# Modulation products of the second layer placed between latent-attention items, their weights split on GpSimd

## The chip, the cores and the metric

The kernel runs on one core of a Trainium2 chip. The metric is device time in microseconds of one execution. The engines are TensorE (PE in the profile; PEld is its weight load), VectorE (DVE), ScalarE (ACT), GpSimd (POOL) and the sequencer that issues most loads (SP).

## What is computed

Two models run one after the other on 512 tokens of width 1024: a block with sparse attention, a memory cross-attention and a feed-forward of width 4096, and then two layers of a mixer that also carry 256 context tokens. The part that the change touches is the modulation of the two mixer layers. It depends on the two condition vectors alone, so it can be computed at any time before its layer uses it:

```python
sc = jax.nn.silu(c)
scc = jax.nn.silu(c_ctx)
for i in range(DEPTH_2):                       # two layers
    mod_x = sc @ w_mod[i] + b_mod[i]           # (1024) x (1024, 3072)
    mod_c = scc @ w_mod[i] + b_mod[i]
    x, ctx = mixer_layer(x, ctx, mod_x, mod_c, ...)
```

In each layer shift and scale of the modulation enter the first norm, and its gate enters the last step. Between them a layer has a window attention, a short convolution, and a latent attention of 8 heads over 768 keys (512 tokens and 256 context tokens).

## The kernel before

All products keep float32 accuracy: each operand is split into a high and a low part, and a product is three matmuls (high by high, low by high, high by low). The kernel is one list of steps, `ops`. Each step is a generator that issues work for one block of weights, and after each piece of it a clock of estimated time (`tick`) lets loads, splits of coming weights and background generators (attention above all) issue theirs. The finished program is then put in order per engine by a scheduler with a timing model of its own, so instructions of neighbouring steps are interleaved, and each engine works through its own fixed order.

Weights come through `Stream`. SP loads chunks of 512 KB into "raw" buffers. `pump` then splits the next unit in stream order into `wh` and `wl`, from a ring of 9 buffers (`RING`). For blocks with `fr=True`, as the modulation's, a unit is 128 rows by 512 columns: ScalarE copies it to `wh` (L266) and VectorE subtracts to get `wl` (L267). Other blocks get float16 halves with a scale; those with `pool=True` have their high half made by GpSimd (L271) and their low half by VectorE (L291).

One modulation product, `mod(i, j, blk)` (L1439), computes 512 of layer `i`'s 3072 columns, for both conditions at once. It takes 8 units. Each has two matmuls over 512 columns, one with 34 stationary columns (L1444 or L1447) and one with 2 (L1445). Then ScalarE and VectorE add the two parts (L1451, L1452) and ScalarE's queue writes the row to DRAM (L1453). After the sixth product of a layer `mod_chain` (L1458) starts: six small loads on ScalarE's queue, a few small VectorE operations (the first is L1469), one matmul and one GpSimd power for a scale (`total`), and three stores to DRAM (L1486). `mod_bc` later reads these with a broadcast load.

Where the 12 products stand is written as the string `MODS`, one letter per product. Before, all six of the second layer (`i` = 1) come first. In order of time: one after the projections of the gating unit (`d`), two after the gating unit (`u`), three while the memory attention runs in the background (`h`). Of the first layer (`i` = 0) one more stands at `h`, two at `i` behind the memory output projection, and three inside the feed-forward (after its parts 0, 1 and 2). After part 4 of the feed-forward `ctx_norm0` norms the context tokens and reads the first layer's modulation for it.

Latent attention is the generator `b_items` (L1932) run by `attention`. For each head it yields five items (four query tiles of 128 over 768 keys, one of two context tiles over 256), and between them small projections: the next head's queries (`qb_head`), the next pair of keys (`kb_pair`), values, gate pieces (`extra`). An item's steps are the score matmuls into one of two PSUM buffers `S`, a maximum on VectorE (L705), an exponential on ScalarE (L721), transposes into one of three PSUM buffers `mm` (L734), a split of these on ScalarE and VectorE (L738, L739), and the value matmuls (L755). All projections and modulation products use the same three `mm` buffers.

## Time and profile before

| | |
|---|---|
| median of 3 runs | 2425.56 us (2424.42 to 2427.5) |
| the profiled execution | 2421.47 us |
| its span, first to last instruction | 2419.7 us |
| PE busy | 2261.3 us, 93% |
| DVE busy | 1544.2 us, 64% |
| ACT busy | 1298.1 us, 54% |
| POOL busy | 320.7 us, 13% |
| mean granted TensorE clock | 0.978 |

The span stands 1.8 us below the time of its own execution, and that execution 4.1 us below the median. Busy shares are means over stages with different limits, so each stage is read by itself. The feed-forward lies at about 480 to 850 us, latent attention of the first layer at about 1165 to 1330 us.

### The profile page before, as it was taken

The page shows a single profiled execution, that of the slowest core. Times are in us where ns is not written, and L with a number is a line of the kernel's source. Part 1 is how long each engine was busy: PE and PEld are TensorE (multiplying, and loading weights), DVE is VectorE, ACT ScalarE, POOL GpSimd, SP SyncE. Part 2 cuts the span into 40 slices and gives each one's busy share as a digit, 9 for nine tenths or more (in the row PEclk, how much of TensorE's full clock was granted, in tenths as well). Part 3 has the DMA queues.
Part 4 walks back from the last instruction along what each step waited for, and adds up shares of the span by engine and source line. Part 5 has one row for each costly group of instructions (what it writes and reads, how often), then busy time and mean ns, then how long its engine had stood idle before and what let it go on. Part 6 is the DMA issues. An engine that isn't in the chain of part 4 may idle for free. (4 is left out here: it accounts for less than half of the span.)

```text
span 2419.7 us, 38066 instructions
## 1 busy us (share of the span) xinstructions
PE 2261.3 (93%) x14342; PEld 1505.2 (62%) x14342; DVE 1544.2 (64%) x3136; ACT 1298.1 (54%) x2745; POOL 320.7 (13%) x703
## 2 busy tenths in 40 slices
PE   7899899899999989999988999999779999899998
PEld 6777687544444557767767566557546567764446
DVE  6878678656665677665777444443777657865543
ACT  5656457746655455535777434323535457775532
POOL 4320321100100211004000000000621121000001
PEclk9899899899999999999999999999989999999999
DMA  4512445534443411112221422211421113233311
GB/s 158 140 47 71 141 144 199 172 101 153 155 140 106 122 50 38 46 40 65 79 74 56 137 79 61 79 42 63 156 86 50 42 38 108 71 115 113 103 44 61
DMA packets 182220, 226.67 MB, mean 94 GB/s; under 512 B 28556, under 2 KB 130876, under 8 KB 182036
## 3 DMA queue, kind: packets, MB, share of 16 engines
q1 hardware_dynamic: 158084, 187.67, 25.1%
q10 hardware_dynamic: 23952, 36.57, 4.4%
q8 instruction: 112, 1.84, 0.3%
q14 instruction: 72, 0.59, 0.1%
HBM read 207.33 MB, written 16.88 MB: 93 GB/s over the span
## 5 line engine op out<-in xcount | busy, mean ns | idle before, releaser
L416 PE MATMUL mm<-hTh,wh 128*128 128x512 f16 (+1 forms) x1040 | 392.6, 378 | 7.3 <-ACT wh L273 3.1
L291 DVE SCALAR_TENSOR_TENSOR wl<-raw,gs,wh 128x512 f16<-128x512 f32 (+2 forms) x420 | 296.6, 751 | 150.6 <-ACT wl L224 116.5
L417 PE MATMUL mm<-hTl,wh 128*128 128x512 f16 (+1 forms) x1040 | 392.4, 377 | 0.0
L418 PE MATMUL mm<-hTh,wl 128*128 128x512 f16 (+1 forms) x1040 | 391.2, 377 | 0.0
L224 ACT ACTIVATE wl<-raw 128x1024 f16<-128x1024 f32 (+3 forms) x242 | 222.9, 921 | 69.6 <-PE mm L417 37.3
L416 PEld LDWEIGHTS <-wh 128*128 128x128 f16 x1712 | 168.0, 98 | 147.4 <-issue 6.8
L417 PEld LDWEIGHTS <-wh 128*128 128x128 f16 x1712 | 168.0, 98 | 146.1 <-issue 9.6
L418 PEld LDWEIGHTS <-wl 128*128 128x128 f16 x1712 | 167.8, 98 | 143.9 <-issue 0.6
L738 ACT ACTIVATE ph<-mm 128x512 f16<-128x512 f32 (+2 forms) x300 | 146.1, 502 | 162.4 <-PE mm L734 156.1
L273 ACT ACTIVATE wh<-raw,gs 128x1024 f16<-128x1024 f32 x156 | 175.3, 1141 | 105.9 <-PE mm L417 83.0
L266 ACT ACTIVATE wh<-raw 128x512 fp32r<-128x512 f32 (+2 forms) x244 | 141.7, 613 | 142.2 <-PE mm L418 49.7
L739 DVE SCALAR_TENSOR_TENSOR pl<-mm,ph 128x512 f16<-128x512 f32 (+2 forms) x300 | 165.9, 567 | 73.6 <-ACT ph L738 71.1
L267 DVE TENSOR_TENSOR wl<-raw,wh 128x512 fp32r<-128x512 f32 (+2 forms) x244 | 156.1, 667 | 55.3 <-ACT wh L266 40.2
L432 POOL TENSOR_TENSOR gs<-gs,nh 128x1 f32<-128x1 f32 x66 | 40.6, 616 | 1125.2 <-DVE gs L431 1079.3
L416 PE MATMUL mm<-wh,hTh 128*128 128x512 f32 (+5 forms) x512 | 181.7, 356 | 5.5 <-DVE vf L1589 2.0
L418 PE MATMUL mm<-wh,hTl 128*128 128x512 f32 (+5 forms) x512 | 180.1, 352 | 1.8 <-DVE hTl L422 1.7
L417 PE MATMUL mm<-wl,hTh 128*128 128x512 f32 (+5 forms) x512 | 180.1, 352 | 0.3 <-DVE wl L267 0.3
L734 PE MATMUL mm<-ident,P 128*128 128x128 f32 x928 | 153.9, 283 | 5.9 <-ACT P L721 2.0
L721 ACT ACTIVATE P<-S,s 128x768 f32<-128x768 f32 (+4 forms) x160 | 105.8, 666 | 35.1 <-PE mm L734 18.0
L734 PEld LDWEIGHTS mm<-ident,P 128*128 128x128 f32 x928 | 108.6, 145 | 19.6 <-ACT P L721 2.9
L2133 DVE SCALAR_TENSOR_TENSOR z<-z,mm 128x256 f32<-128x256 f32 (+1 forms) x72 | 42.8, 596 | 107.2 <-PE mm L418 98.9
L271 POOL TENSOR_SCALAR wh<-raw,gs 128x1024 f16<-128x1024 f32 (+3 forms) x54 | 65.8, 1219 | 328.2 <-PE mm L417 209.9
(503 smaller groups left out, 5360.8 us busy)
## 6 DMA issues: line engine op xcount, KB each, us to landing
raw<-in_w_in_dram SPq DMA_DIRECT2D x124, 512.0 KB, 3.5
raw<-in_w_ff_dram SPq DMA_DIRECT2D x64, 512.0 KB, 4.5
raw<-in_w_mod_dram SPq DMA_DIRECT2D x48, 512.0 KB, 5.1
raw<-in_w_branch_dram SPq DMA_DIRECT2D x24, 512.0 KB, 3.4
raw<-in_w_o_dram SPq DMA_DIRECT2D x16, 512.0 KB, 4.0
raw<-in_cmp_w_dram SPq DMA_DIRECT2D x16, 256.0 KB, 3.5
raw<-in_w_out_dram SPq DMA_DIRECT2D x8, 512.0 KB, 3.6
raw<-in_w_mkv_dram SPq DMA_DIRECT2D x8, 512.0 KB, 3.7
```

The costliest lines, as they stand in the source:

```text
L224: nc.scalar.activation(lo[:, :b - a], t[:, a:b], AF.Square, accum_out=g.t[:, g.cols:g.cols + 1])
L266: nc.scalar.activation(hi[:, :m], src, AF.Copy)
L267: nc.vector.tensor_sub(lo[:, :m], src, hi[:, :m].bitcast(FT))
L273: nc.scalar.activation(hi[:, :m], src, AF.Copy, scale=s)
L291: self.nc.vector.scalar_tensor_tensor(l[:, b], src[:, b], s, h[:, b], op0=OP.mult, op1=OP.subtract)
L416: PE.matmul(ps, ah, bh, start=start, stop=False)
L417: PE.matmul(ps, ah, bl, start=False, stop=False)
L418: PE.matmul(ps, al, bh, start=False, stop=stop)
L721: ACT.activation(P, v[:, j, :], AF.Exp, bias=it.nb[:, j:j + 1], accum_out=it.den[:, j:j + 1])
L734: PE.transpose(ps[:, a - a0, :], it.P[0 if len(it.P) == 1 else j][:, c:c + 128], ident)
L738: ACT.activation(ph[:, :m], ps[:, :m], AF.Copy, scale=PSC)
L739: DVE.scalar_tensor_tensor(pl[:, :m], ps[:, :m], PSC, ph[:, :m], op0=OP.mult, op1=OP.subtract)
```

## The change

The change moves modulation products. `MODS` becomes six letters and lists the first layer alone: two products at `u`, two at `h`, two at `i`; none at `d` and none in the feed-forward. The six of the second layer go into the latent attention of the first layer, heads 1 to 6, product `j` = head minus 1. `mod` can now run a part of its 8 units: units 0 to 3 follow the item (head, query tile 1), units 4 to 7 the item (head, query tile 3). Its PSUM buffer is taken at unit 0 and kept to unit 7. These blocks have `pool=True`, and for them both halves of the split are GpSimd's, a copy for `wh` and a subtraction for `wl`. The small operand `s1` moves to a pool that lives through the whole kernel.

```diff
-MODS = 'duuhhhhii012'
+MODS = 'uuhhii'
@@ Stream.pump
+        elif fr and u.blk.pool:
+            nc.gpsimd.tensor_copy(hi[:, :m], src)
+            nc.gpsimd.tensor_tensor(lo[:, :m], src, hi[:, :m].bitcast(FT), op=OP.subtract)
         elif fr:
             nc.scalar.activation(hi[:, :m], src, AF.Copy)
             nc.vector.tensor_sub(lo[:, :m], src, hi[:, :m].bitcast(FT))
@@ mod_init
-        s1 = sc["one"].tile([128, 8, 34], FR, tag="ms1", name="ms1")
+        s1 = one.tile([128, 8, 34], FR, tag="ms1", name="ms1")
@@
-    def mod(i, j, blk):
-        ps = mmtile([128, 512])
-        for k in range(8):
+    def mod(i, j, blk, ks=range(8)):
+        if ks[0] == 0:
+            lay["mps"] = mmtile([128, 512])
+        ps = lay["mps"]
+        for k in ks:
...
+        if ks[-1] < 7:
+            return
@@
-    def b_items(nq, segs, blks, extra):
+    def b_items(nq, segs, blks, extra, mods):
...
+                if h in mods and qt in (1, 3):
+                    yield proj_item(mod(1, h - 1, mods[h], range(qt * 2 - 2, qt * 2 + 2)))
@@ layer
+        md = {j + 1: wblk(A["w_mod_2"][1][:, j * 512:(j + 1) * 512], fr=True, pool=True) for j in range(6)} if i == 0 else {}
...
+            bl += [md[h]] if h in md else []
@@
-    mods = [(n, (1, n) if n < 6 else (0, n - 6)) for n in range(12)]
+    mods = [(n, (0, n)) for n in range(6)]
```

## Rows read from the trace of the kernel before

**Rows 1.** Stretch, length; busy PE, PEld, DVE, ACT, POOL (instructions); clock; DMA share, GB/s.

```profile
500.00:660.00 160.00, 159.27 (x742) 71.53 (x741) 92.58 (x178) 97.27 (x172) 8.79 (x14) 1.00 0.41 126
370.00:425.00 55.00, 52.58 (x394) 39.84 (x393) 49.39 (x88) 41.92 (x96) 7.00 (x18) 0.97 0.67 227
1165.00:1200.00 35.00, 33.20 (x263) 27.52 (x261) 23.92 (x51) 25.46 (x72) 0.69 (x1) 1.00 0.23 68
1200.00:1322.00 122.00, 104.11 (x791) 87.56 (x790) 94.34 (x182) 88.65 (x191) 3.88 (x6) 0.96 0.22 69
```

**Rows 2.** Waits of PE in latent attention, 1165 to 1345 us: total, times, longest.

```profile
PE S L416 <- ACT P L721: 12.1, 11, 2.5
PE O L755 <- DVE yb L2009: 2.8, 3, 2.1
```

**Rows 3.** Timeline of PE around a product in the feed-forward: start, duration, instruction.

```profile
623.83 0.38 PE L417 MATMUL mm<-wl,ffh 128*128 128x512 f16 x1
624.05 0.38 PE L418 MATMUL mm<-wh,ffl 128*128 128x512 f16 x1
...
627.97 0.39 PE L416 MATMUL mm<-hTh,wh 128*128 128x512 f16 x1
```

**Rows 4.** Timelines of ACT's queue, DVE and PE where the context norm starts.

```profile
652.77 1.42 ACTq L1486 DMA_DIRECT2D mod_d<-mf  x1
...
660.78 1.28 DVE L618 SCALAR_TENSOR_TENSOR xn<-ctx,s,g 128x1024 f32<-128x1024 f32 x1 [4.00 <-DMA g<-mod_d]
...
654.85 0.38 PE L416 MATMUL mm<-wh,ffh 128*128 128x512 f16 x1 [0.73 <-DVE oc L1240]
663.12 0.38 PE L416 MATMUL mm<-wh,ffh 128*128 128x512 f16 x1 [2.93 <-DVE oc L1240]
```

**Rows 5.** Timelines of DVE and PE at the end of the memory attention.

```profile
411.34 4.88 DVE L267 TENSOR_TENSOR wl<-raw,wh 128x512 fp32r<-128x512 f32 x8
417.55 0.68 DVE L1452 TENSOR_TENSOR z<-mm,z 2x512 f32<-2x512 f32 x1
418.16 4.89 DVE L267 TENSOR_TENSOR wl<-raw,wh 128x512 fp32r<-128x512 f32 x8
...
419.60 0.39 PE L1447 MATMUL mm<-wh,ms 128*34 128x512 f32 x1
420.18 0.48 PE L416 MATMUL mm<-wh,moh 128*128 128x512 f32 x1
```

**Rows 6.** Busy time by stretch, at the product `d` and just behind it.

```profile
230.00:240.00 10.00, 9.64 (x121) 6.62 (x119) 9.61 (x15) 9.33 (x20) 0.00 (x0) 1.00 0.62 196
250.00:260.00 10.00, 6.07 (x44) 3.88 (x43) 4.74 (x9) 4.76 (x13) 4.49 (x15) 0.79 0.00 0
```

**Rows 7.** What VectorE's first operation of the modulation chain (L1469) waited for.

```profile
  DMA raw<-in_w_mod_dram: 3.5, 1
  DMA mf<-raw_d: 2.4, 1
```

**Rows 8.** GpSimd's wide operations, by form: count, busy us and mean ns, idle before.

```profile
L271 POOL TENSOR_SCALAR wh<-raw,gs 128x1024 f16<-128x1024 f32 x40 | 53.0, 1328 | 222.0 <-PE mm L417 127.6 <-PE mm L418 69.1 <-issue 24.4
...
L271 POOL TENSOR_SCALAR wh<-raw,gs 128x576 f16<-128x576 f32 x2 | 1.5, 748 | 7.0 <-PE mm L417 7.0
```

**Rows 9.** Timelines of POOL and DVE in the window attention, where both work at once.

```profile
876.84 3.20 POOL L271 TENSOR_SCALAR wh<-raw,gs 128x1024 f16<-128x1024 f32 x2 [18.36 <-PE mm L418]
915.65 1.12 POOL L271 TENSOR_SCALAR wh<-raw,gs 128x1024 f16<-128x1024 f32 x1 [3.60 <-PE mm L417]
...
876.94 0.42 DVE L1549 TENSOR_TENSOR y<-z,ra 128x256 f32<-128x256 f32 x1
877.28 1.26 DVE L1550 TENSOR_TENSOR y<-z,ra 128x256 f32<-128x256 f32 x1
...
902.61 0.15 DVE L1659 TENSOR_TENSOR s<-nb,sk 128x4 f32<-128x4 f32 x1
...
915.95 0.83 DVE L1659 TENSOR_TENSOR s<-nb,sk 128x4 f32<-128x4 f32 x1
```

**Rows 10.** VectorE groups with two SBUF inputs, 1200 to 1322 us: the largest two.

```profile
L291 DVE SCALAR_TENSOR_TENSOR wl<-raw,gs,wh 128x512 f16<-128x512 f32 x18 | 12.7, 746 | 0.7 <-ACT wl L224 0.7
L1863 DVE TENSOR_TENSOR qb<-y,qb 128x512 fp32r<-128x512 f32 x5 | 3.4, 681 | 0.0
```

More of the change, by code (lines that the diff above doesn't have):

```diff
@@ L2277, in layer @@
             bl += [za[f] for f in range(4) if zh.get(f) == h]
-        add(lambda *b: attention(b_items(nq, segs, [x for x in b if x not in za], zat)), *bl)
+            bl += [md[h]] if h in md else []
+        other = za + list(md.values())
+        add(lambda *b: attention(b_items(nq, segs, [x for x in b if x not in other], zat, md)), *bl)
         add(lambda: s4_start())
```

## The prediction

> **What bounds the kernel now.** I read first the busy time by stretch, then in each stretch that the change touches PE's waits and the timelines of the engines beside it. The feed-forward is bound by PE: 159.27 us of 160 [rows 1]. The end of the memory attention is bound by VectorE and PE together (49.39 and 52.58 of 55 us), and the stretch with the product at `d` likewise [rows 1, 6]. Latent attention is different: from 1200 to 1322 us PE works 104.11 of 122 us (85%), VectorE 94.34, ScalarE 88.65, and GpSimd 3.88 [rows 1]. Its largest wait is of score matmuls for the exponential that frees their PSUM buffer, 12.1 us in 11 pieces, none longer than 2.5 [rows 2]. So that stage has holes in PE and an idle GpSimd, and the feed-forward has neither; the question is how much of the moved work falls into the holes.
>
> **What a product costs on PE.** From one float16 matmul's start to the next is 0.22 us. From the last one before the third product to the first behind it is 3.92 us [rows 3]. So the product's 16 matmuls take 3.92 - 0.22 = 3.70 us, and six take 22.2 us.
>
> **Removed from the feed-forward.** Three products on a busy PE: 3 x 3.70 = 11.1 us. Their splits, loads and sums lie beside PE work and give nothing more. Bounds 9 to 11.3 (below 11.1 if the scheduler's new order opens small holes).
>
> **The wait of the context norm.** The first layer's modulation is now finished before the feed-forward. In the trace the chain's last store is issued at 652.8 us, VectorE stands 4.00 us for the broadcast load from it, and two matmuls then wait 0.73 and 2.93 us for sums queued behind that on VectorE [rows 4]. The 3.66 us should go; what is late next there are the context rows' own load and the norm, so I take 3.3, bounds 1 to 3.7.
>
> **Removed at `h` (four products to two).** Behind the memory attention's last values VectorE does two runs of 8 subtractions, 4.88 and 4.89 us, with 0.68 between, and PE's next projection starts at 420.18, right behind the fourth product [rows 5]. Two products cost 2 x 3.70 = 7.4 us on PE and about 2 x (4.9 + 0.7) = 11.2 us on VectorE. The stage is near the limit of both, so the gain lies between; but with fewer products beside it, attention's own chain shows. I take 8, bounds 4 to 11.
>
> **Removed at `d` (one product to none).** PE 9.64 and VectorE 9.61 of 10 us there [rows 6], so 3.7 us of PE or 5.6 us of VectorE. But right behind it PE is busy 6.07 of 10 [rows 6]: norm chains set the pace, and what is won may be waited away. I take 3, bounds 0 to 5. The products at `u` and `i` keep their places and only change layer.
>
> **The chain of layer one moves to the start of the feed-forward.** Its first VectorE operation waited 2.4 and 3.5 us for loads in its two uses [rows 7], with weight splits queued behind it. Bounds 0 to 3.5; the nearer use is the one inside the feed-forward, where PE still worked 159.27 of 160 us [rows 1]; I take 0.5.
>
> **Added to latent attention.** Each product brings 16 matmuls, 8 copies and 8 subtractions on GpSimd, one ScalarE copy, one VectorE add, one store on ScalarE's queue, and four loads of 512 KB on SP. The 24 loads are 12.6 MB; over some 135 us that is 93 GB/s on top of 69. The memory attention ran at 227 GB/s [rows 1], so I cost them at nothing; without that cover GpSimd's copies would wait for them.
>
> *PE.* 104.1 + 22.2 = 126.3 us of work. If every hole fills, the 122 us become 126.3: +4.3. If none fills: +22.2. The nearest row is the same stage's beginning, 1165 to 1200, where gate pieces lie between the items: PE 33.20 of 35, 94.9% [rows 1]. At that share 126.3 / 0.949 = 133.1: **+11.1**.
>
> *GpSimd's time.* Nothing in the trace shows a copy or a two-input subtraction of 512 columns there. The one-input operation takes 0.748 us for 576 columns and 1.12 undisturbed for 1024 [rows 8, 9], so 0.83 ns a column and about 0.70 us for the copy. The subtraction is bounded below by the same 0.70 and above by twice it, 1.40; with two inputs to fetch I take the upper, about 2.1 us a unit, 101 us for 48. They may begin in head 0, as far as the ring of 9 allows, so there are about 130 us: enough, if waits stay below 0.6 us a unit. Waits for the five small powers queued behind them are inside this.
>
> The Trainium skill (GPSIMD Engine Reference, Engine selection) speaks against the change: two-input elementwise work belongs on VectorE, and its cycle accounting gives some 2.6 cycles an element, by which I estimate 1.1 us for the subtraction. By it the unit is 1.8 us and the sum does not change.
>
> *VectorE beside GpSimd.* A 4-element VectorE operation with two SBUF inputs took 0.83 us instead of 0.15 while GpSimd's wide one ran; a 256-column one took 1.26 instead of 0.42; and GpSimd's two beside it took 3.20 instead of 2.24 [rows 9]. They exclude each other. From 1200 to 1322 us VectorE has 34 such operations (18 and 5 in the largest groups [rows 10]). With GpSimd busy some 80%, and half of about 1 us left on average, each waits 0.4 us: 14 us more on an engine that has 28 idle. Most are weight splits ahead of need, five are queries that scores wait for. I take **+3**, bounds 0 to 8.
>
> *The rest.* The chain of the second layer now runs at head 6: six loads and three stores on ScalarE's queue, and VectorE's wait of 2.4 to 3.5 us [rows 7] with maxima queued behind: **+1.5**, bounds 0 to 3.5. A product keeps one of three `mm` buffers from tile 1 to tile 3; transposes and key projections have two meanwhile. No row shows that; PE's waits on these buffers are small against those for `S` [rows 2], so **+1**, bounds 0 to 4.
>
> **The sum**, against the profiled execution of 2421.47 us: removed 11.1 + 3.3 + 8 + 3 = 25.4; added 0.5 + 11.1 + 3 + 1.5 + 1 = 17.1; net -8.3. The median stands 4.1 us above that execution, and I let the difference stand: 2425.56 - 8.3 = **2417**. With all parts at their best it would be 31 less against 4.3 more, 2399; at their worst 14 less against 41 more, 2453.
>
> **Rivals.**
> (a) *The holes fill almost wholly*, because the scheduler may put a ready product ahead of a score matmul that waits. For it: the holes are 1 to 2.5 us [rows 2] and half a product is 1.85. Against it: the order is fixed by a model, and real waits fall elsewhere. Then 4.3 + 2.5 is added and 25.4 removed: 2407. Chance 0.22.
> (b) *Little is won before the feed-forward.* The norm chains and the attention's own chain are as long without the products. For it: the idle behind `d` [rows 6]. Against: VectorE near full at both places. Then only 14.4 is removed against 17.1: 2428. Chance 0.20.
> (c) *GpSimd becomes the bound of latent attention (slower).* If a unit with its waits takes over (122 + 11 + 8) / 48 = 2.9 us, PE waits for weights in its fixed order. At 3.3 us the 48 take 158 us instead of 130, VectorE's collisions grow to 8, and the sum is -25.4 + 28 + 8 + 1.5 + 1 + 0.5 = +13.6: 2439. For it: the mutual exclusion [rows 9], by which a copy of 1.12 became 1.6. Against: at 2.1 us a unit there is 30% to spare. Chance 0.13. The Trainium skill's rule above points to this side; by its own figure the unit stays below the limit.
>
> **How the numbers follow.** Main case 0.45, centred on 2417, 2409 to 2425. I give 2403 to 2432: it holds the main case, nearly all of (b) and most of (a), and leaves out (c) and the far end of (a). About 0.2% (4.9 us) is what a measurement of this kernel can tell from no change. Faster by more: most of the main case and (a), 0.60; within: 0.23; slower: (c) and the upper part of (b), 0.17.
>
> **What the changed profile would show.** Feed-forward some 14 us shorter with no wait on a load from the modulation. The stretch from the last memory-attention values to the output projection shorter by about 7. Latent attention some 16 us longer with PE at 93 to 96% in its middle; if PE stays at 85%, no hole was filled. GpSimd's copies near 0.7 and subtractions at or below 1.4 us, with PE seldom waiting for them; many such waits mean (c). Waits of transposes for an `mm` buffer would show the PSUM term too small. The forecast is wrong if the stages before the feed-forward keep their length, or if latent attention grows by over 25 us.

## The result and the profile after

The changed kernel takes 2441.16 us, the kernel before, measured beside it, 2426.53: a ratio of 1.0059, 95% interval 1.0042 to 1.0077. It is slower by some 14.6 us, where 2417 and a range of 2403 to 2432 were forecast. The profiled execution took 2440.92 us (span 2439.1), that of before 2421.47 (span 2419.7); their spans differ by 19.4 us, since the profiled execution of before lay some 5 us under its median. The ledger below is between these two.

Where the time went is read from the same instruction in both traces. The sums of the feed-forward's second product first, in the kernel before (the two figures behind the durations are the first and the last start):

```profile
L1240 DVE SCALAR_TENSOR_TENSOR oc<-mm,gs,oc x64: 737/750/753, 516.1 to 825.6; 128x512 f32<-128x512 f32 x64
```

The same in the changed kernel:

```profile
L1243 DVE SCALAR_TENSOR_TENSOR oc<-mm,gs,oc x64: 736/750/754, 513.2 to 805.9; 128x512 f32<-128x512 f32 x64
```

The changed kernel is 2.9 us ahead at the first of these sums and 19.7 ahead at the last: the feed-forward is 16.8 us shorter. The same reading at other places: 6.5 us ahead at the first operation behind `d` (246.0 to 239.5), 5.4 at the first sum of the output projection (292.3 to 286.9), 7.6 at the last sum behind the memory attention (445.4 to 437.8), 4.9 at the feed-forward's first activation (478.2 to 473.3). Most of the gain of 19.7 is kept as far as latent attention, whose first maximum stands 18.3 us earlier. Then all of it is lost and more.

The rows of stretches answer to [rows 1] and [rows 4]: the changed kernel's feed-forward, the place where the context norm starts, and latent attention over the same times as before's [rows 1].

```profile
500.00:660.00 160.00, 160.00 (x750) 72.61 (x748) 91.31 (x169) 85.80 (x125) 5.39 (x9) 1.00 0.34 112
640.00:680.00 40.00, 40.00 (x188) 18.12 (x187) 21.51 (x38) 21.61 (x32) 0.55 (x1) 1.00 0.32 105
1165.00:1322.00 157.00, 131.53 (x906) 99.39 (x906) 111.69 (x197) 96.16 (x225) 87.18 (x91) 0.97 0.36 115
```

PE is now never idle where it waited 3.66 us for the context norm. In latent attention it works 131.53 of 157 us, 84%, where before it worked 33.20 + 104.11 = 137.31 of the same stretch [rows 1]: 22 us of matmuls (by the forecast's price) were added to the stage, which is also longer, and this stretch of it became emptier.

Latent attention is measured from VectorE's first maximum to its last output sum, and the ends of the first three of its four head pairs are the second reciprocal of each. These are rows of VectorE's timeline, of the kernel before:

```profile
1160.91 0.95 DVE L705 TENSOR_REDUCE s<-S 128x1 f32<-128x768 f32 x1
1202.88 0.18 DVE L2013 RECIPROCAL s<-dn 128x4 f32<-128x4 f32 x1
1248.14 0.17 DVE L2013 RECIPROCAL s<-dn 128x4 f32<-128x4 f32 x1
1297.60 0.17 DVE L2013 RECIPROCAL s<-dn 128x4 f32<-128x4 f32 x1
1335.44 0.42 DVE L2009 TENSOR_TENSOR yb<-O,yb 64x256 f32<-64x256 f32 x1
```

and of the changed kernel:

```profile
1142.62 0.96 DVE L708 TENSOR_REDUCE s<-S 128x1 f32<-128x768 f32 x1 [0.81 <-PE S L421]
1187.24 0.15 DVE L2022 RECIPROCAL s<-dn 128x4 f32<-128x4 f32 x1
1238.68 0.17 DVE L2022 RECIPROCAL s<-dn 128x4 f32<-128x4 f32 x1
1295.29 0.17 DVE L2022 RECIPROCAL s<-dn 128x4 f32<-128x4 f32 x1
1352.52 0.42 DVE L2018 TENSOR_TENSOR yb<-O,yb 64x256 f32<-64x256 f32 x1
```

The stage is 174.5 us before and 209.9 after: **35.4 us longer**. The pairs take 42.0, 45.3, 49.5 and 37.8 before, 44.6, 51.4, 56.6 and 57.2 after. Behind it little is added: the changed kernel is 17.1 us late at the stage's end, 18.3 at the first merge and 19.4 at its own end.

PE's waits in latent attention, 1165 to 1345 us, answer to [rows 2]:

```profile
PE S L419 <- ACT P L724: 7.2, 6, 3.2
PE mm L419 <- DVE pl L742: 6.3, 7, 2.7
PE mm L737 <- DVE pl L742: 3.9, 3, 2.2
PE O L758 <- ACT ph L741: 3.8, 6, 1.8
PE mm L433 <- DVE sb L431: 2.8, 2, 2.2
PE mm L2029 <- DVE pl L742: 1.4, 2, 0.8
```

PE waits no longer mostly for the exponential but for `mm` buffers that VectorE's `pl` (the low half of the transposed exponentials) frees: 11.6 us in the second, third and sixth row. No wait of PE for GpSimd stands in the whole list. GpSimd's own groups in the stage:

```profile
L267 POOL TENSOR_TENSOR wl<-raw,wh 128x512 fp32r<-128x512 f32 x45 | 58.8, 1320 | 0.5 <-ACT wl L224 0.3
L266 POOL CAST wh<-raw 128x512 fp32r<-128x512 f32 x45 | 30.7, 692 | 74.4 <-PE mm L420 27.9 <-PE mm L1452 17.5 <-PE mm L1449 10.0
```

A unit takes 0.69 + 1.32 = 2.01 us, as forecast (2.1), and GpSimd is idle 74.4 us before its copies, 55.4 of them until PE frees a ring buffer. So it is late for nobody that the profile names, and still the stage is 35 us longer. That is what the experiments are about.

### The profile page after: what moved, and what is told of

Its sections match the earlier page's. It is cut to its first block, busy times and chain, and to the rows that moved or that the text cites. A ratio compares the mean times of both kernels' runs of the same rounds, so it can differ in the third digit from the quotient of the medians.

```text
span 2439.1 us, 38037 instructions
## 1 busy us (share of the span) xinstructions
PE 2276.1 (93%) x14342; PEld 1515.8 (62%) x14342; DVE 1532.3 (63%) x3088; ACT 1273.9 (52%) x2673; POOL 415.7 (17%) x799
## 3 DMA queue, kind: packets, MB, share of 16 engines
q1 hardware_dynamic: 158084, 187.67, 24.9%
## 4 chain that ended last, share of the span: by engine, by line
PE 78%; DVE 8%; ACT 5%; DMA 3%; issue 3%; POOL 2%; SPq 0%; ACTq 0%; DVEq 0%; POOLq 0%
PE mm L419 22%; PE mm L420 21%; PE mm L421 21%; PE mm L737 3%; PE O L758 2%; DVE wl L294 2%; ACT P L724 1%; DVE pl L742 1%; ACT wl L224 1%; ACT ph L741 1%; PE S L419 1%; PE S L633 1%; DMA raw<-in_w_in_dram 1%; PE S L421 1%; PE S L420 1%
## 5 line engine op out<-in xcount | busy, mean ns | idle before, releaser
L435 POOL TENSOR_TENSOR gs<-gs,nh 128x1 f32<-128x1 f32 x66 | 40.6, 616 | 975.4 <-DVE gs L434 917.9
L269 ACT ACTIVATE wh<-raw 128x512 fp32r<-128x512 f32 (+2 forms) x196 | 114.5, 610 | 89.3 <-PE mm L420 20.1
L270 DVE TENSOR_TENSOR wl<-raw,wh 128x512 fp32r<-128x512 f32 (+2 forms) x196 | 126.1, 669 | 30.6 <-ACT wh L269 29.0
L708 DVE TENSOR_REDUCE s<-S 128x1 f32<-128x768 f32 (+4 forms) x112 | 97.5, 874 | 22.2 <-PE S L421 14.5
```

Of the source, the lines that this page charges most:

```text
L269: nc.scalar.activation(hi[:, :m], src, AF.Copy)
L270: nc.vector.tensor_sub(lo[:, :m], src, hi[:, :m].bitcast(FT))
```

## The experiments

Each figure called "stage" is the length just defined, in the profiled execution of that kernel. Kernels that leave part of the splitting out have other values in the second layer's modulation. Each stage length comes from one execution; four kernels that leave the stage as it was (the kernel before among them) have 174.4 to 175.6, so a difference of 1 to 2 us says nothing.

### What is it: buffers, splits or matmuls?

**A PSUM buffer for each half.** The half is closed with its own copy, add and store:

```diff
-        if ks[0] == 0:
-            lay["mps"] = mmtile([128, 512])
-        ps = lay["mps"]
+        ps = mmtile([128, 512])
...
```

> Each half product of the second layer gets its own PSUM buffer and is closed at once (one copy, one add, one store more per product; the chain loads both halves and adds them). The changed kernel took 2441 us, and its first latent attention grew from 174 to 210 us. Theory 'hold' (a product keeps one of three mm buffers for 17 to 22 us, so transposes and projections wait): the waits for mm buffers fall from about 20 to under 8 us, the stage to about 198, the time to 2428 to 2433. Theory 'collisions' (VectorE and GpSimd exclude each other): stage 208 to 212, time 2438 to 2444. Theory 'added work' (the matmuls fill no hole): the same, 2438 to 2444.

2438.14 us, ratio 1.0044 [1.0029, 1.0060]; stage 208.0, 1.9 less. From first matmul to copy the six products keep buffers for 80 us in all instead of 115, and others of PE's waits take the place of those for `mm` buffers. Two rows of its stage:

```profile
PE O L758 <- ACT ph L741: 8.9, 4, 4.4
PE mm L737 <- DVE pl L742: 2.7, 4, 0.8
```

The waits of `mm` for `pl` are 4.1 us in all instead of 11.6, the wait for `ph` 8.9 instead of 3.8. Not keeping the buffer across the gap brings almost nothing.

**The product whole, behind tile 1.**

```diff
-                if h in mods and qt in (1, 3):
-                    yield proj_item(mod(1, h - 1, mods[h], range(qt * 2 - 2, qt * 2 + 2)))
+                if h in mods and qt == 1:
+                    yield proj_item(mod(1, h - 1, mods[h]))
```

> The eight units of a product lie together behind tile 1 of a head instead of four behind tile 1 and four behind tile 3, so its PSUM buffer is kept some 6 us instead of 17 to 22. Theory 'hold': the stage goes from 210 to about 200 us, the time to 2430 to 2434. Theory 'collisions' and theory 'added work': no change, 2438 to 2444. Theory 'GpSimd's pace' (eight units at about 2 us each have to be split ahead): PE waits for splits and the time is 2441 to 2450.

2441.87 us, 1.0055 [1.0033, 1.0077]; stage 213.5. It did not do what it was made for: the matmuls were spread over as long as before (107 us of keeping). It only shows that the arrangement in halves matters little.

**One split in eight.** The other pieces reuse the first one's split.

```diff
+        again = fr and u.blk.pool and u.ks[0] > 0
+        if again:
+            hi, lo = u.blk.of[0][0].hi, u.blk.of[0][0].lo
...
```

> GpSimd splits only the first of the eight weight pieces of each second-layer product; the other seven matmul pairs use that split again, so 42 of 48 copies and subtractions are left out (the second layer's modulation has other values than the reference's). Matmuls, loads, buffers and their order stay. Theory 'collisions': VectorE's operations return to their durations of the kernel before, the stage goes from 210 to about 195 us, the time to 2424 to 2430. Theory 'hold' or 'added work': stage 206 to 210, time 2437 to 2442. Theory 'GpSimd's pace': as 'collisions', but then PE's waits, not VectorE's busy time, are what falls.

2412.90 us, 0.9937 [0.9917, 0.9958]; stage 185.4. All matmuls, loads and stores are there, and the stage is only 10.9 us longer than before. **The 42 splits left out cost 24.5 of the 35.4 us.** The time is below the 2424 that any theory gave, and the buffers are now kept for 37 us: GpSimd's work, the waiting and the keeping went together, so the run names the splits and not the way they cost. Part of that way can be read. The stage with one split in eight, and in the changed kernel (columns as in the rows of stretches above):

```profile
1142.78:1328.19 185.41, 169.21 (x1277) 133.10 (x1275) 135.85 (x274) 129.75 (x298) 13.09 (x16) 0.99 0.36 108
1142.62:1352.52 209.90, 178.82 (x1280) 138.23 (x1279) 151.26 (x280) 132.19 (x304) 91.87 (x97) 0.95 0.36 112
```

Of the 24.5 us PE is idle for 14.9, and for 9.6 it is longer at work on nearly the same number of matmuls. The added idle time is mostly waiting for VectorE, 18.5 us instead of 5.2; of these the waits of `mm` for `pl` are 11.6 us instead of 1.6, while those for the exponential stay. With one split in eight:

```profile
PE S L425 <- ACT P L730: 7.4, 8, 2.0
PE mm L743 <- DVE pl L748: 0.8, 4, 0.3
PE mm L425 <- DVE pl L748: 0.5, 1, 0.5
PE mm L2035 <- DVE pl L748: 0.3, 1, 0.3
```

In these waits of the changed kernel VectorE is at work for 18.1 of the 18.5 us. One of the two longest, of 2.2 us, ends with the second of these rows of VectorE's timeline:

```profile
1257.80 3.26 DVE L1919 TENSOR_TENSOR wl<-raw,wh 128x288 fp32r<-128x288 f32 x3
1261.75 0.41 DVE L742 SCALAR_TENSOR_TENSOR pl<-mm,ph 128x256 f16<-128x256 f32 x1
```

There `pl` stands in VectorE's order behind three splits of query weights. Beside GpSimd's work they took 1.50 us (288 columns) and twice 0.96 (48 columns); in the kernel before such splits take 0.45 and 0.20.

The longer work of PE goes with its granted clock, 0.95 of full speed (2.4 GHz) over the stage instead of 0.99. Behind the stretch with that wait, in which PE worked 2.10 of 4.30 us and VectorE 4.09, the clock fell to 1.2 GHz:

```profile
1259.00:1263.30 4.30, 2.10 (x16) 1.37 (x16) 4.09 (x7) 0.40 (x1) 4.30 (x5) 1.00 0.36 111
1263.30:1266.70 3.40, 3.11 (x16) 2.34 (x16) 1.60 (x3) 1.96 (x5) 3.35 (x3) 0.50 0.98 325
1266.70:1272.00 5.30, 5.25 (x50) 4.74 (x49) 3.39 (x6) 3.02 (x10) 0.00 (x0) 1.00 0.98 325
```

No run holds the clock fixed, so how many of the 9.6 us are its doing is not shown.

**Keeping a buffer alone**, in the kernel before:

```diff
+                if 1 <= h <= 6 and qt == 1 and nq == 6:
+                    lay["mps"] = mmtile([128, 512])
+                    PE.transpose(lay["mps"][:1, 0:128], st["den"][:, 1, h % 2:h % 2 + 1], ident)
+                if 1 <= h <= 6 and qt == 3 and nq == 6:
+                    PE.transpose(lay["mps"][:1, 128:256], st["den"][:, 3, h % 2:h % 2 + 1], ident)
...
```

> The kernel before, and in the first latent attention one of the three mm buffers is taken behind tile 1 of heads 1 to 6 and given back behind tile 3 (two transposes of one column and a one-element copy per head, nothing else). Theory 'hold': latent attention grows from 174 to 182 to 188 us, the time by 8 to 14 us. Theory 'collisions' or 'added work': the time grows by at most 2 us.

2439.57 us, 1.0053 [1.0039, 1.0067]; stage 190.0, 15.5 longer (a profiled execution 7 us above its median). A buffer taken from the attention is dear by itself. But own buffers, kept for 80 us instead of 115, gave back only 1.9 us of the changed kernel's 35.4.

**The last split first.** Own buffer for each half, and its matmuls begin with the piece that is split last, so that they can run together:

```diff
+        order = [ks[-1], *ks[:-1]] if i else list(ks)
+        for k in order:
...
```

> The changed kernel with a PSUM buffer for each half product (closed with one copy, one add and one store of its own, as in the run with own buffers), and the half's last split used first, so that its matmuls start when all four splits are there. Measured so far from a product's first matmul to its copy, summed over six: changed kernel 115 us, own buffers 80, one split 37, and the stage 209.9, 208.0, 185.4 us; a buffer kept for nothing in the kernel before lengthened the stage by 15.5. Theory 'hold paced by GpSimd' (the buffer is kept for as long as GpSimd needs to deliver the splits): sum of holds 25 to 40, stage 190 to 198 us, time 2420 to 2430. Theory 'collisions' (wide GpSimd operations hold VectorE up; 15.7 us in the changed kernel) or 'ring and order': stage 204 to 212, time 2434 to 2444.

2448.72 us, 1.0110 [1.0080, 1.0141]; stage 217.9. The expected shortening failed: the scheduler again spread the matmuls (96 us of keeping), and the stage grew. Over the kernels with products the stage follows the keeping only roughly: 37 us of it go with 185.4 (and 185.1), 44 with 194.2, 49 with 207.3 and with 212.1 (kernels below, whose products run in one piece), 80 with 208.0, 96 with 217.9, 107 with 213.5, 115 with 209.9, 120 with 216.8, 132 with 217.3, 154 with 255.2. From 49 to 115 it hardly grows; below that, the splitting was cut as well.

### Is it VectorE, held up by GpSimd?

**GpSimd's work alone**, in the kernel before, first without anything to wait for:

```diff
...
+                if 1 <= h <= 6 and qt < 4 and nq == 6:
+                    for _ in range(2):
+                        for _ in range(2):
+                            POOL.tensor_copy(gx, gx)
+                        for _ in range(2):
+                            POOL.tensor_tensor(gx, gx, gx, op=OP.subtract)
```

> The kernel before, and in heads 1 to 6 of the first latent attention GpSimd does as many columns of copies and subtractions as the changed kernel's 42 to 48 splits, on a tile of its own that nobody reads (two units behind each of the tiles 0 to 3; nothing waits for them). The one-split run gave 28 us of the changed kernel's time to GpSimd's splits. Theory 'collisions' (VectorE's operations are held up while GpSimd works): VectorE's busy time in the stage rises by 15 us or more, the stage grows from 174 to 185 to 195 us, the time by 10 to 20 us. Theory 'pace' (matmuls stand in a fixed order behind splits that come late): the stage stays within 3 us, the time within 4 us of the kernel before.

2428.39 us, 1.0014 [1.0004, 1.0025]. It says nothing on the question: with nothing to wait for, the operations ran ahead of the stage, which took 175.6 (the row gives the first and the last start):

```profile
L1971 POOL TENSOR_TENSOR gx<-gx x96: 607/614/1471, 839.2 to 1040.6; 128x256 f32<-128x256 f32 x96
```

**The same, held back to its place:** a first copy of one column reads the tile's sums of exponentials.

```diff
...
+                    POOL.tensor_copy(gx[:, 0:1], st["den"][:, qt, h % 2:h % 2 + 1])
...
```

> The kernel before with GpSimd's 48 units of copies and subtractions on a tile of its own, as in the run that let GpSimd run ahead, but now each pair of units waits for the exponentials of its tile of attention, so that the work lies in heads 1 to 6 of latent attention. Theory 'collisions': VectorE's busy time in the stage rises by 15 us or more, the stage from 174 to 185 to 195 us, the time to 2435 to 2445. Theory 'late splits': stage up to 178, time within 4 us of the kernel before.

2448.91 us, 1.0098 [1.0069, 1.0126], which looks like the collisions; the profile says otherwise. The stage took 179.6, 5.1 longer, and VectorE's work in it rose by 2.9 us (134.1 against 131.2). The rest came behind the stage: GpSimd was still at its backlog, and ScalarE stood 27.3 us for one load instead of 4.5 (`ACT yhl L681 <- DMA xn<-yc_d`); what held the load up I did not follow. A total without its stages would have misled here.

**Once more, with operations 512 wide and free in time** (heads 1 to 5; `gi` reads a 128-column constant four times, and the results have half the width in bytes, so the subtraction takes 1.07 us):

```diff
...
+                if 1 <= h <= 5 and qt < 4 and nq == 6:
+                    POOL.tensor_copy(gx[:, 0, 0:1], st["den"][:, qt, h % 2:h % 2 + 1])
+                    for _ in range(2):
+                        POOL.tensor_copy(gx, gi)
+                        POOL.tensor_tensor(gx, gi, gi, op=OP.subtract)
```

> The kernel before with 40 units of one 512-column copy and one 512-column subtraction on GpSimd, two behind each of the tiles 0 to 3 of heads 1 to 5, each pair held back until its tile's exponentials are done; operations as wide as the changed kernel's, and GpSimd free again before the stage ends (the earlier run of this kind used 256 columns and left a backlog at the stage's end). Theory 'collisions' (VectorE's two-input operations wait for GpSimd's, so the wider the worse): VectorE's busy time rises by 8 to 15 us, the stage from 174.5 to 184 to 195 us, time 2434 to 2445. Theory 'buffers and order': up to 178 us, time within 4 us of the kernel before.

2429.92 us, 1.0022 [1.0007, 1.0038]; stage 180.3, 5.8 longer, VectorE 3.7 us longer at work. In these two runs GpSimd works about as long in the stage as in the changed kernel (94.8 and 78.5 us against 91.9), and collisions alone cost 5 to 6 us, not 25. But they hold VectorE up for 3 to 4 us only, where the changed kernel has 15.4 us more VectorE work than with one split in eight; so the two runs do not bound what 15 us of it would cost.

**VectorE's time alone**, 48 subtractions more in the kernel before:

```diff
...
+                if 1 <= h <= 6 and qt < 4 and nq == 6:
+                    for _ in range(2):
+                        DVE.tensor_tensor(gx, gi, gi, op=OP.subtract)
```

> The kernel before with 48 subtractions of 512 columns more on VectorE (about 0.68 us each, 33 us in all), two behind each of the tiles 0 to 3 of heads 1 to 6 of the first latent attention, on data that is always there and for nobody. From the first maximum to the last output sum the kernel before takes 174.5 us there, the changed kernel 209.9. Theory 'VectorE's time' (whatever keeps VectorE longer, its own work or GpSimd's, lengthens the stage nearly one for one): 195 to 208 us, time 2444 to 2458. Theory 'buffers and order' (the splits cost through the ring of buffers and the fixed order, and VectorE has room): up to 184 us, time up to 2434.

2437.83 us, 1.0046 [1.0028, 1.0064], and inconclusive for the same reason as the first GpSimd run. The row of the added line shows when they ran:

```profile
L1968 DVE TENSOR_TENSOR gx<-ident x48: 672/688/1369, 839.1 to 914.0; 128x512 f16<-128x512 f32 x48
```

Free of waits, the scheduler put all 48 into the window attention, 320 us too early. The stage itself stayed at 174.4. (Where they landed they cost some 11 us by the ratio, 15 by the start of latent attention in the two profiled executions; that says something of that stage alone.)

**GpSimd's work in place.** The one-split kernel, and GpSimd copies and subtracts the other 42 pieces on the loaded weights themselves, for nobody:

```diff
+        elif again:
+            nc.gpsimd.tensor_copy(src, src)
+            nc.gpsimd.tensor_tensor(src, src, src, op=OP.subtract)
...
```

> The one-split kernel (2413 us), but GpSimd does the copy and the subtraction of the other 42 pieces in place on the loaded weights: the same GpSimd work at the same time, loads that wait for it, and nobody who needs its result (the second layer's modulation has other values than the reference's). Theory 'late splits' (PE stands in a fixed order behind the splits and their ring): 2413 to 2418 us, latent attention as with one split. Theory 'collisions' (VectorE is held up by GpSimd), or loads held up by GpSimd: 2433 to 2442 us; in the first case VectorE's busy time in the stage rises from 136 to about 150 us.

2442.46 us, 1.0073 [1.0053, 1.0093], and again the stage contradicts the total: it took 185.1, as with one split, while GpSimd worked 43 us in it. With only their loads to wait for, 25 of the 42 pieces ran ahead of the stage. The loss lies there, where GpSimd's small operations for a norm stood behind this work in its queue and PE waited for the norm. Waits of PE, 1110 to 1172 us:

```profile
PE S L640 <- DVE xn L628: 15.4, 4, 12.3
```

So the part of GpSimd's work that did stand beside the stage was cheap where nobody needed it; VectorE's work in the stage rose by 1.2 us only.

**The subtraction in four pieces of 128 columns:**

```diff
-            nc.gpsimd.tensor_tensor(lo[:, :m], src, hi[:, :m].bitcast(FT), op=OP.subtract)
+            for a in range(0, m, 128):
+                b = slice(a, a + 128)
+                nc.gpsimd.tensor_tensor(lo[:, b], src[:, b], hi[:, b].bitcast(FT), op=OP.subtract)
```

> The changed kernel with each of GpSimd's subtractions of 512 columns done as four of 128: the same work, loads, buffers and matmuls, but an operation of some 0.34 us instead of 1.28 for a VectorE operation to run into. In the runs so far the stage grew by 1.3 to 1.9 us for each microsecond by which GpSimd held VectorE up (changed kernel: 15.7 held up, 24.5 longer than with one split). Theory 'collisions': held-up time falls from 15.7 to 4 to 7 us, the stage from 209.9 to 192 to 200, the time to 2423 to 2432. Theory 'buffers and order', or GpSimd's total time: no gain, stage 206 to 214, time 2437 to 2445.

2446.84 us, 1.0085 [1.0065, 1.0105]; stage 216.8. The operations that were to be held up less were. VectorE's splits of 48 columns, in the kernel before:

```profile
L1912 DVE TENSOR_TENSOR wl<-raw,wh 128x48 fp32r<-128x48 f32 x6 | 1.0, 199 | 0.0
```

in the changed kernel:

```profile
L1919 DVE TENSOR_TENSOR wl<-raw,wh 128x48 fp32r<-128x48 f32 x10 | 7.5, 790 | 0.0
```

and with four pieces:

```profile
L1921 DVE TENSOR_TENSOR wl<-raw,wh 128x48 fp32r<-128x48 f32 x10 | 2.7, 311 | 0.0
```

The time for which one VectorE operation is held up follows the length of one GpSimd operation, and yet the stage became 6.9 us *longer*, while VectorE's work in all of it fell from 151.3 to 146.7 us. That speaks against collisions as the main cause, and the kernel below that splits on ScalarE and VectorE, without GpSimd, refutes it: I had formed that theory from six runs in which held-up time and stage rose together. GpSimd's unit had meanwhile grown:

```profile
L269 POOL TENSOR_TENSOR wl<-raw,wh 128x128 fp32r<-128x128 f32 x187 | 84.7, 488 | 1.2 <-ACT wl L224 0.9
L266 POOL CAST wh<-raw 128x512 fp32r<-128x512 f32 x46 | 28.8, 635 | 58.9 <-PE mm L422 24.0 <-PE mm L1451 13.6 <-issue 11.0
```

to 0.635 + 4 x 0.488 = 2.59 us, so shorter operations and more GpSimd time came together.

**In sixteen pieces of 32 columns**, the same edit with 32 in place of 128:

> As before, with sixteen subtractions of 32 columns each (about 0.1 us apiece, GpSimd's unit some 2.3 to 2.7 us instead of 1.9). Theory 'collisions': held-up time 2 to 5 us, stage 188 to 198, time 2420 to 2431, unless GpSimd's longer unit makes PE wait (then PE waits for GpSimd show). Theory 'buffers and order': stage 206 to 216, time 2437 to 2447.

2479.61 us, 1.0227 [1.0211, 1.0242]; stage 255.2. The pieces took 265 ns each, not 100, and the unit 0.636 + 16 x 0.265 = 4.88 us. Here, and only here, PE's waits name GpSimd:

```profile
L269 POOL TENSOR_TENSOR wl<-raw,wh 128x32 fp32r<-128x32 f32 x733 | 166.2, 265 | 0.0
PE mm L1452 <- POOL wl L269: 27.0, 14, 3.5
```

### Who splits, and how much

**ScalarE and VectorE**, as all other weights:

```diff
-        md = {j + 1: wblk(..., fr=True, pool=True) for j in range(6)} if i == 0 else {}
+        md = {j + 1: wblk(..., fr=True) for j in range(6)} if i == 0 else {}
```

> The changed kernel with the second layer's weights split as all others are: copy on ScalarE, subtraction on VectorE; GpSimd has no part in it. VectorE gets 48 subtractions of about 0.6 us (29 us), ScalarE 48 copies. Theory 'collisions': the 22 us of held-up VectorE time go and 29 us of work come, so the stage is 200 to 212 us and the time 2430 to 2443. Theory 'pace': PE no longer waits on late splits, VectorE at 150 of some 190 us carries the work, the stage is 186 to 195 us, the time 2415 to 2425.

2438.48 us, 1.0051 [1.0034, 1.0069]; stage 207.3. Without GpSimd the splits cost 21.9 us more than with one in eight, so GpSimd is not needed for the loss.

**ScalarE copies, GpSimd subtracts:**

```diff
-            nc.gpsimd.tensor_copy(hi[:, :m], src)
+            nc.scalar.activation(hi[:, :m], src, AF.Copy)
```

> The changed kernel with the copy of each second-layer split on ScalarE and only the subtraction on GpSimd: GpSimd's work falls from 1.95 to 1.3 us a unit. Either theory expects a gain of about a third of the 28 us that the splits cost: stage near 202 us, time 2430 to 2434. If only the two-input operation collides with VectorE, the gain is under 3 us (2438 to 2442).

2438.01 us, 1.0054 [1.0039, 1.0069]; stage 212.1. A third of GpSimd's time taken off, and put on ScalarE, gains nothing.

**Splits of 34 columns.** Each matmul takes the small result as its stationary side and the product's first piece as its moving side, so that waits and ring buffers stay:

```diff
+            m = 34 if u.ks[0] > 0 else m
...
+            if i == 1 and k:
+                sh, sl = wh[:, 0:34], wl[:, 0:2]
+                wh, wl = lay["w0"]
...
```

> The changed kernel with GpSimd's copy and subtraction of 42 of the 48 pieces cut from 512 columns to 34; each matmul takes the small result as its stationary side, so that it still waits for its own split and ring buffer, and the first piece of the product as its moving side (other values in the second layer's modulation). Theory 'late splits' by their work, or 'collisions': 2412 to 2418 us. If the ring of nine buffers, which the product's pieces occupy, is what costs (buffers and not work): 2433 to 2442 us.

2420.37 us, 0.9984 [0.9974, 0.9994]; stage 194.2. Waits and ring with little work cost 8.8 us over one split in eight; with the full work it is 15.7 more.

Set in order of the time of a unit (durations from each trace, on whichever engine):

| a unit is split in | by | stage |
|---|---|---|
| (one in eight) | GpSimd | 185.4 |
| 0.25 + 0.28 = 0.53 us | GpSimd, 34 columns | 194.2 |
| 0.62 + 0.68 = 1.30 | ScalarE, VectorE | 207.3 |
| 0.62 + 1.33 = 1.95 | ScalarE, GpSimd | 212.1 |
| 0.69 + 1.32 = 2.01 | GpSimd (changed kernel) | 209.9 |
| 0.64 + 1.95 = 2.59 | GpSimd, 4 pieces | 216.8 |
| 0.64 + 4.24 = 4.88 | GpSimd, 16 pieces | 255.2 |

Six of the 48 units are split in every kernel of the table, so its first row is the start for the other 42. From it to 2.59 us the stage grows by 31.4 us. For each microsecond of those 42 splits that is 0.39, 0.40, 0.33, 0.29 and 0.29 us in the rows from 0.53 to 2.59: **0.3 to 0.4 of the time of the splits comes back as length of the stage, whoever does them and though PE waits, by the profile, for none of them**. The growth is not even (1.95 us go with a longer stage than 2.01). At 4.88 us, where PE does wait for them, it is 0.34.

### What the stage did before, and a faster kernel

In the kernel before, the same engines also read ahead the next stage's weights here, with squares and copies on ScalarE and subtractions on VectorE. In the changed kernel the products stand first in the one ordered stream, and 18 of these subtractions, 8 copies and 13 squares fall into the last pair, which is 19.4 us longer. **Two runs on that.** The kernel before, with the reading ahead held back until head 6 (`hold` is the stream's last chunk of the attention's own):

```diff
...
+        if self.hold is not None and ci > self.hold and not must:
+            self.finish()
+            return False
...
+            if h == 6:
+                stream.hold = None
...
```

> The kernel before, and the reading ahead of the next stage's weights (squares and copies on ScalarE, subtractions on VectorE) is held back during the first latent attention until head 6; no product is moved. In the kernel before, the four head pairs end 42.0, 45.3, 49.5 and 37.8 us after one another (the last up to the last output sum); in the changed kernel 44.6, 51.4, 56.6 and 57.2. Theory 'displaced reading ahead' (the products' pieces stand first in the one ordered stream, so the next stage's 18 subtractions, 8 copies and most of 17 squares fall into the last pair): pairs one to three as before or up to 4 us shorter, the last 46 to 56, time 2432 to 2442. Theory 'splits and buffers alone': the last pair up to 41, time 2423 to 2429.

2417.65 us, **0.9972 [0.9960, 0.9985]: faster than both kernels, and than either theory allowed.** The last pair did grow, by 9.2 to 47.0. But the first three fell by 1.9, 3.4 and 8.8, the third by more than the 4 us that were allowed, and the stage is 169.6. Busy time by pairs, of this kernel:

```profile
1157.61:1197.67 40.06, 38.75 (x302) 32.20 (x301) 30.17 (x59) 27.52 (x76) 0.00 (x0) 1.00 0.24 77
1197.67:1239.52 41.85, 37.74 (x293) 33.04 (x294) 28.44 (x58) 32.00 (x77) 0.55 (x1) 0.96 0.05 17
1239.52:1280.17 40.65, 38.72 (x299) 31.40 (x299) 30.93 (x55) 28.30 (x64) 0.00 (x0) 1.00 0.12 37
1280.17:1327.20 47.03, 37.47 (x304) 31.52 (x303) 41.56 (x90) 36.88 (x71) 4.30 (x6) 0.93 0.43 130
```

and of the kernel before:

```profile
1160.91:1202.88 41.97, 39.03 (x296) 31.50 (x294) 29.65 (x64) 31.37 (x91) 0.69 (x1) 1.00 0.20 61
1202.88:1248.14 45.26, 38.72 (x297) 32.86 (x298) 35.35 (x73) 33.36 (x73) 2.78 (x4) 1.00 0.21 65
1248.14:1297.60 49.46, 41.90 (x301) 33.95 (x300) 36.50 (x67) 35.77 (x73) 0.55 (x1) 0.93 0.24 71
1297.60:1335.44 37.84, 34.29 (x303) 30.11 (x302) 29.67 (x57) 25.76 (x57) 0.55 (x1) 0.95 0.20 62
```

In the second and third pair VectorE does 28.44 and 30.93 us instead of 35.35 and 36.50, and PE passes nearly the same matmuls (293 and 299 instead of 297 and 301) in 12.2 us less. 3.2 of these in the third pair are PE's own work, at a granted clock of 1.00 instead of 0.93. Here too a stage in which VectorE has 10 to 13 us idle in a pair runs faster when VectorE is spared 6 to 7.

The changed kernel with no reading ahead until the attention is issued whole, the same edit with the hold lifted at its end:

> The changed kernel, and the next stage's weights are not read ahead before the first latent attention has been issued whole; products, splits, loads and buffers of the products stay. Theory 'displaced reading ahead': the last pair falls from 57.2 to 38 to 44 us, the first three stay at 44.6, 51.4, 56.6; up to 10 us come back between the last output sum and the first merge (25.1 in the changed kernel); time 2426 to 2436. Theory 'splits and buffers alone': the last pair stays above 52 us and the time is 2438 to 2450.

2446.42 us, 1.0090 [1.0068, 1.0111]; stage 217.3. The last pair did not fall to 44 (64.6 to the last output sum), and 27.7 us instead of 25.1 lie behind it. So the displaced reading ahead is not what makes the changed kernel slow: the first run shows that it is a gain by itself. The second adds less, since in it PE waits 11.6 us in one piece for a sum of squares of a gate weight (`PE mm L437 <- DVE sb L435`), which the held-back stream delivers late.

### The two layers exchanged in the kernel before

```diff
-    mods = [(n, (1, n) if n < 6 else (0, n - 6)) for n in range(12)]
+    mods = [(n, (n // 6, n % 6)) for n in range(12)]
```

> The kernel before with the two layers' products exchanged in their twelve places: the first layer's six come first, the second layer's last. It keeps all matmuls and splits in place and has, of the change, only that the first layer's modulation is finished before the feed-forward. If the context norm's wait is all that this brings: 3.3 us less, 2421 to 2425. If the chain at the start of the feed-forward is what cost the changed kernel some 4.7 us there: no gain, 2425 to 2429.

2422.00 us, 0.9992 [0.9981, 1.0003]: no difference that can be told. Its sums of the feed-forward, beside those shown first:

```profile
L1240 DVE SCALAR_TENSOR_TENSOR oc<-mm,gs,oc x64: 730/750/752, 518.5 to 825.1; 128x512 f32<-128x512 f32 x64
```

The first is 2.4 us later than in the kernel before, the last 0.5 earlier. The context norm's wait is won (2.9 us), and the first layer's chain at the feed-forward's start takes 2.4 of it back.

## Why the prediction was wrong

**The feed-forward: right.** Forecast 11.1 + 3.3 = 14.4, measured 16.8. With the products left in place, the context norm's part alone is 2.9. The three products and the wait are 14.0 of the 16.8; where the other 2.8 come from I did not look.

**`h` and `d`: right in sum within the bounds, wrong in place.** Forecast 8 and 3, measured about 2.2 (7.6 less 5.4) and 5.4 to 6.5, so 7.6 of 11. At `h` I took a value between PE's and VectorE's load. Whether the attention's own chain, which I named, sets the pace there is not shown: between the two places PE still works 147.2 of 150.9 us (149.9 of 152.7 before), because other matmuls, those of the next product among them, moved in front of the second place. So the division between this term and the next one is rough.

**The chain of layer one at the feed-forward's start: too small.** Forecast 0.5, bounds up to 3.5; measured 7.6 - 2.9 = 4.7, and 2.4 with the layers exchanged. The nearer row was not the one that I chose but the start, where I take it that the splits queued behind the chain are wanted at once. PE's waits, 430 to 480 us, of the changed kernel:

```profile
PE mm L1450 <- DVE wl L270: 3.9, 1, 3.9
...
PE mm L419 <- ACT wh L276: 2.8, 1, 2.8
PE S L433 <- DVE sb L431: 2.5, 2, 1.9
```

In sum 18.3 us were won up to latent attention's first maximum, 24.9 were forecast: rival (b) in part.

**PE's matmuls in latent attention: right in sum.** Forecast +11.1, with 1 for the buffer and 1.5 for the chain, so 13.6. With one split in eight the stage is 10.9 longer, for all three. But there, as in the changed kernel, the reading ahead has gone to the last pair, which by itself shortens the stage by 4.9 us (169.6). Against that stage the products cost 15.8. The +1 for the buffer is doubtful alone: a buffer kept for nothing cost 15.5, outside the bounds of 0 to 4.

**The step that failed is "VectorE beside GpSimd +3", and with it everything that I let the splits cost: 24.5 us for 42 of them.** The amount of held-up time was not the error: 14 us were forecast, and VectorE's work is 15.4 us longer than with one split in eight (151.26 and 135.85 in the rows above). The errors were to set them against "28 us idle" and keep 3, and to have no other term for the splits, which cost 21.9 us on ScalarE and VectorE, where GpSimd has no part in them. The mean idle share was no room. From 1259 to 1263.3 us, shown above, VectorE works 4.09 of 4.30 us and PE 2.10, and in PE's waits for VectorE, which are what grew, VectorE is nearly always at work. I read it thus: in a chain of maximum, exponential, transposes, splits and products, with three `mm` buffers and a fixed order, an engine is often idle because it waits its turn, and what is put on it there pushes the next turn. The sum also had no term for PE's clock, which was granted lower in the longer waits (0.95, against 0.97 before and 0.99 with one split in eight).

**Rival (c) gave 2439 and came near by accident.** Its mechanism, PE waiting for GpSimd from 2.9 us a unit, is not what happened: at 2.01 and 2.59 us no wait of PE names GpSimd, at 4.88 us 27.0 us do. Its point of decision, 2.9 us, lies between these and is not refuted; the cost begins long before it.

**The signs to look for.** "Latent attention longer by over 25" and "PE stays at 85%" both came. "Waits of transposes for an `mm` buffer" came too: transposes and projections wait 11.6 us for `pl` in the rows above instead of 1.4. But own buffers took most of these waits away and brought 1.9 us back: I would have read that sign wrongly. Among the rivals, (a) leaves out the 3 and the 0.5 without a reason; with them it gives 2410.

**What stays open.** That the splits cost 24.5 us, and that it grows with their time, is shown. It reaches PE as 14.9 us of waiting, mostly for VectorE's `pl`, and as 9.6 us of longer work at a lower clock. What makes `pl` late is shown for single waits only: where the splits run on GpSimd VectorE is held up, where they run on VectorE it has more to do, and when these waits were taken away (own buffers) others came up. Keeping a buffer cost 15.5 alone, but own buffers returned only 1.9; the ring's order with small splits is worth up to 8.8. The scheduler gives each of these kernels another order of the stage, and no run separates that from the work.

## What to carry to other kernels

Before work is moved into a stage with holes, look at why the holes are there: where several engines hand one tile round, an idle share is not room, and each microsecond of work that the chain depends on costs a fraction of itself (here 0.3 to 0.4 for the splits, on GpSimd as on ScalarE and VectorE). Take the same rule the other way: moving optional work *out* of such a stage (here the reading ahead of later weights, held back to its last quarter) made this kernel faster by 0.28%. And measure an added load only where it is tied to its place by data, and by its stage: of the five kernels here with work added for nobody, two ran it in another stage, one held up small operations behind it, and one left a backlog.

## What the runs showed of the hardware

The time that a VectorE operation loses follows the length of the single GpSimd operation that it meets: a split of 48 columns took 199 ns alone, 790 beside GpSimd operations of 1.32 us, 311 beside those of 0.49. The Trainium skill (SBUF — State Buffer, SBUF: two separate sides) says that GpSimd and a VectorE operation with two SBUF inputs, as this subtraction has, take a shared pair of ports by an exclusive lock for a whole instruction, and that the loser blocks. These rows agree.

GpSimd's two-input operation took 265 ns for 32 columns, 488 for 128 and 1320 for 512: some 2.2 ns a column above 0.2 us of its own, so cutting it small is dear. The Trainium skill (GPSIMD Engine Reference, Elementwise — side-by-side cycle accounting) has two figures for such an operation, 2.6 cycles an element and 4497 ns for 2048 columns. The second is 2.2 ns a column, as here; the first gave the forecast's estimate of 1.1 us for 512 columns, which lacks the 0.2 us.

TensorE's granted clock fell to 1.2 GHz behind a stretch in which PE worked 2.10 of 4.30 us, and rose to 2.4 GHz again behind 3.40 us in which it worked 3.11. The transposes of the exponentials, in an earlier such stretch of the changed kernel (1205.3 to 1208.5 us) and at full clock (1170 to 1200 us):

```profile
L737 PE MATMUL mm<-ident,P 128*128 128x128 f32 x4 | 1.1, 421 | 0.0
L737 PE MATMUL mm<-ident,P 128*128 128x128 f32 x32 | 5.1, 278 | 2.5 <-ACT kst L1894 1.3 <-DVE pl L742 1.2
```

They take 421 ns instead of 278. So a wait can cost more than its own length.
